# A hand-written instruction order, exchanged for the first periods of a matrix product

## The chip, the cores and the metric

The kernel runs on one core of a Trainium2 chip. The metric is the device time of one execution in microseconds (us). The engines are called as in the profile: PE multiplies matrices, DVE and ACT do elementwise work, POOL does little here, and SP issues every DMA of this kernel. Each engine works through its own list of instructions in order; an instruction that waits holds up all that stands behind it on the same engine.

## The reference

```python
def reference(x, w):
    cs = np.cumsum(x, axis=1)
    diff = cs - np.concatenate([np.zeros(...), cs[:, :-1, :]], axis=1)
    return np.matmul(diff, w).astype(np.float32)
```

x is 8 x 2048 x 2048 and w is 2048 x 2048, both float32 standard normal. The differences of a cumulative sum are the numbers that were summed, so the result is x times w: 16384 rows of 2048, each a product with the same w.

## The kernel before

**Tiles and periods.** The 16384 rows are 128 tiles of 128 rows. The first four (PLAIN = 4) are multiplied plainly, in bf16, while w is still arriving. The others go in groups of four tiles through a two-level product of the Strassen-Winograd kind in f16, which replaces matmuls on PE by additions on DVE. The work is recorded in periods: period 0 has the four plain tiles and the first group (tiles 4 to 7), period k the group of tiles 4 + 4k to 7 + 4k. Within a period a tile is called by its role: 0 to 3 are the tiles of the period's own group, 4 to 7 those of the next group, 8 and up those behind.

**Order by hand.** Every operation is first recorded with a label and an engine (L117), with no order. Then emit (L205) sorts all recorded operations by 1620 times the period plus a place, looked up by label in the table `places` (L1184 on), and each engine is given its operations in that order (after, L98). The table has an entry for periods 0, 1, 2, 29, 30 and 31, and one for all between (None). A place may be negative or over 1620: then the operation is sorted in among those of the period before or after. So the table alone sets what stands before what on PE, DVE, ACT and on SP's queue of DMAs. Waits for data follow from the tiles that are read and written.

**The head (period 0).** SP loads x tiles of the first four rows ("first x.q.a", L254; q is a quarter of the columns, a one of two pairs of rows) and w pieces ("w.h.ko", L295: half h of the columns, 128 rows ko). On DVE each x tile is cast to bf16 ("cast x", L260), PE transposes it with eight small matmuls ("turn x", L269), and DVE or ACT copies the result back ("turned x", L279). Each piece of w is cast to bf16 ("cast w", L313, on ACT) into one of seven buffers and used by the plain matmuls ("plain.h.r.ko", L324); "left over" (L476) is the last small product of that phase. Before the first data arrive, PE runs dummy matmuls on zeros ("warm", L362).

**The scale of w.** DVE takes the maximum of each piece of w ("max w", L305), then the maximum over these ("max", L447); POOL takes it over the partitions, and DVE forms uw and its reciprocal uinv (L453, L454). With uinv DVE and ACT scale w into f16 blocks B11, B21, B22 and so on (L460, L462), from which the blocks T1 to T4 and the second-level operands ("inK.make..", "inK.Q..", L576) are subtracted on DVE.

**A group's x.** For a tile of role r: load r (SP, L132), weigh r (ACT, sums of absolute values, L140), mean r (ACT, L161), scale r (DVE, reciprocal, L163), narrow r.i (ACT, to f16, L178), turn r.i (SP, a DMA that transposes from the staging buffer F into the x operands, L195). Each comes in two halves i. S1g, S1h, S2h, S3h and S4h are sums of x tiles on DVE (L576). S1h of a period subtracts the tiles of its roles 2 and 3, which are roles 6 and 7 of the period before.

**A group's products.** P1 to P5 are products with second-level operands. PN.0 to PN.6 are their quarter matmuls on PE (L610; four matmuls each) and some plain products are issued by L588. PN.s1 to PN.s4 are subtractions on DVE for operands; PN.first, PN.out2 and PN.out4 are copies on ACT (L627); PN.middle and PN.last are DVE's. Results are first kept by ACT ("keep", L624) and then added to by DVE ("C11g+P2.g.0" and the like, L635), each sum in two halves. When both halves of a sum are done, SP stores it ("put r.h", L643).

**SP.** All DMAs of the kernel stand in one queue in the order of the table. A DMA that waits, for instance a store for its sum, holds those behind it.

Of the kernel before, what the change touches and what calls it, by code (L numbers as in the profile page):

```python
# [10 lines left out]
def kernel(  # L11
# [30 lines left out]
    WARM = 30  # L42
# [72 lines left out]

    def record(label, engine, ask):
# [56 lines left out]
    def narrow_one(t, i):  # L173
        to, data, s = narrowed(t)[:, ds(i * NH, NH)], where[t][i], scales[t]
        record(
            f"narrow{role(t)}.{i}",
            "act",
            lambda: nc.scalar.activation(to, data, COPY, scale=s),  # L178
        )
        if i == 1 and t != PLAIN + 1:  # L180
            stage.append(where[t][1])
# [75 lines left out]
    def cast_x(q, a):  # L257
        to = resting(q, 0).bitcast(bf16).rearrange("p (a c) -> p a c", a=2)[:, a]
        src = resting(KH - 1 - q, a)
        record(f"cast x.{q}.{a}", "dve", lambda: nc.vector.tensor_copy(to, src))  # L260
        return to
# [13 lines left out]
    def turned(q, a, v, engine):  # L275
        to = xP[:, ds(2 * a, 2), ds(q * KQ, KQ), :].rearrange("p r k m -> p r (k m)")
        v = v.rearrange("p (r c) -> p r c", r=2)
        on = nc.scalar.copy if engine == "act" else nc.vector.tensor_copy
        record(f"turned x.{q}.{a}", engine, lambda: on(to, v))  # L279
# [30 lines left out]
    def taken(h, ko):  # L310
        src = rest(h, ko)
        to = wb[h, ko] = next(rings)
        record(f"cast w.{h}.{ko}", "act", lambda: nc.scalar.copy(to, src))  # L313
        largest(h, ko)
# [22 lines left out]
    def result(name, p, rows, columns, u=None):  # L337
        c = next(results_at)
        if u is None and name in ("out.0.1.0", "out.0.2.0"):
            record(f"{name}", "dve", lambda: nc.vector.tensor_copy(c, p))  # L340
        elif u is None:
            record(f"{name}", "act", lambda: nc.scalar.copy(c, p))  # L342
        else:
            record(f"{name}", "act", lambda: nc.scalar.activation(c, p, COPY, scale=u))
# [52 lines left out]
    for ko in range(KO - KQ):  # L397
# [20 lines left out]
        if ko == PART[-1]:  # L418
            for k in PART:
                part(k)  # L420
            record("part", "act", lambda: nc.scalar.copy(partial, banks[7]))
# [35 lines left out]
    def block(name, dst, a, h, k, engine):  # L457
        to, src = dst[k], whole[k][:, a, h, :].rearrange("p (n c) -> p n c", c=NB)
        if engine == "dve":
            ask = lambda: nc.vector.tensor_scalar(to, src, uinv, None, MUL)  # L460
        else:
            ask = lambda: nc.scalar.activation(to, src, COPY, scale=uinv)  # L462
        record(f"{name}.{k}", engine, ask)
# [159 lines left out]
    def keep_one(label, c, p, u):  # L623
        record(label, "act", lambda: nc.scalar.activation(c, p, COPY, scale=u))  # L624

    def copy(label, to, p):
        record(label, "act", lambda: nc.scalar.copy(to, p))  # L627
# [188 lines left out]

    def group_plain(g):
# [69 lines left out]
        make_2(in_2)  # L887
# [16 lines left out]
        make_3(in_3)  # L904
# [18 lines left out]
    def all_seven(g):  # L923
        return g > PLAIN + 4

# [3 lines left out]
    def first_two(g):  # L929
        if g < END:  # L930
# [3 lines left out]
            if all_seven(g):  # L934
# [3 lines left out]
            ready[2] = Quarters("P2", ready["zz"], A12g, A12h, in_2, room(at + 1), False)  # L938

    def group(g):  # L940
        h = g + 2
        more = all_seven(g)
# [30 lines left out]
        if more:  # L973
# [29 lines left out]
        P5 = Quarters("P5", P2.banks, S1g, S1h, in_5, room(at))  # L1003
# [12 lines left out]
        if not more:  # L1016
            make_5(in_5)
        in_5.give("Q3")
# [15 lines left out]
        if not more:  # L1034
            make_1(in_1)
# [7 lines left out]
        P3 = Quarters("P3", P5.banks, S4g, S4h, in_3, room(at + 1))  # L1043
# [12 lines left out]
        in_3.give("Q1")  # L1056
# [20 lines left out]
        P4 = Quarters("P4", P3.banks, A22g, A22h, in_4, room(at))  # L1077
        P4.one()
        P4.two()
        in_3.give("Q3")  # L1080
        if not more:
            make_3(in_4)
# [19 lines left out]
        in_4.give("Q1")  # L1102
# [19 lines left out]
        in_4.give("Q3")  # L1122
# [25 lines left out]
        if next_g < END:  # L1148
            if all_seven(g + 4):
# [12 lines left out]
        P4.slot(6)  # L1162
        turn(next_l, [1])
# [13 lines left out]
    for g in range(PLAIN + 4, END, 4):  # L1177
# [8 lines left out]
            'first x.0.2': 0, 'first x.1.1': 1, 'first x.0.0': 2, 'first x.1.3': 3,  # L1186
            'first x.0.3': 4, 'first x.0.1': 5, 'first x.1.2': 6, 'first x.1.0': 7, 'w.0.0': 8,
            'zeros': 9, 'least': 10, 'ones': 11, 'numbers': 12, 'numbers turned': 13, 'eye': 14,
# [394 lines left out]
```

## Time and profile before

| | |
|---|---|
| time, median of 3 runs | 1450.54 us (1450.36 to 1450.79) |
| the profiled execution's span, first to last instruction | 1449.2 us |
| its clock of PE, mean granted | 0.999 of full speed |
| DMA | 351.59 MB, mean 243 GB/s |
| instructions | 20358, of which PE 6692, DVE 2345, ACT 1994 |

The span leaves out what lies before the first and behind the last instruction; the median of the runs is 1.3 us above it. In the profile a row of the timeline gives the start in us, the time to the end of the last of its instructions, engine, line, operation, what is written from what, the count, and in brackets how long the engine was idle before the first of them and who ended that wait. A row of the windows gives for a stretch of time its length and, for each engine, the busy us with the count of instructions, then the granted clock of PE, the share of time that the DMA engines were busy, and GB/s. A row of a group gives count, busy us, the mean of one in ns, the idle time before them and who ended most of it.

The chain of work that ended last is 91% on PE: 61% on L610 and 30% on L588.

### The profile page before, as it was taken

To read this page: it belongs to the slowest core of one execution; us is meant where nothing else is said; L and a number is where in the kernel's file an instruction comes from. 1 tells how busy PE (TensorE), PEld (TensorE's weight loads), DVE (VectorE), ACT (ScalarE), POOL (GpSimd) and SP (SyncE) were. 2 spreads that over 40 slices of the span, in tenths; PEclk is the share of its full clock that TensorE was granted. 3 is DMA by queue.
4 is the path that set the end of the run, shared out by engine and by line. 5 is a ranking of instruction groups with operands and counts; after the bars stand their busy time and mean duration, and the time that the engine had idled before them with its cause. 6 is when DMAs were issued, how large, how long until landed. Compare 5 with 4: busy or idle time off the path is not lost.

```text
span 1449.2 us, 20358 instructions
## 1 busy us (share of the span) xinstructions
PE 1438.6 (99%) x6692; PEld 652.2 (45%) x6698; DVE 1334.3 (92%) x2345; ACT 1204.5 (83%) x1994; POOL 0.5 (0%) x5
## 2 busy tenths in 40 slices
PE   8999999999999999999999999999999999999998
PEld 4444444444444444444444444444444444444443
DVE  6999999999999999999999999999999999999988
ACT  5997888898888888888988888988888888889783
POOL 0000000000000000000000000000000000000000
PEclk9999999999999999999999999999999999999999
DMA  9999979899888999989998888998989998989973
GB/s 360 369 252 272 252 212 228 240 247 262 226 234 226 243 262 231 244 222 228 247 265 233 228 229 237 252 257 226 222 239 244 260 248 225 218 236 248 264 200 116
DMA packets 343930, 351.59 MB, mean 243 GB/s; under 512 B 270992, under 2 KB 270992, under 8 KB 343824
## 3 DMA queue, kind: packets, MB, share of 16 engines
q1 hardware_dynamic: 343824, 350.29, 89.4%
q8 instruction: 52, 0.85, 0.2%
q14 instruction: 54, 0.44, 0.1%
HBM read 150.99 MB, written 134.22 MB: 197 GB/s over the span
## 4 chain that ended last, share of the span: by engine, by line
PE 91%; issue 4%; DMA 2%; ACT 2%; DVE 1%; DVEq 0%; POOLq 0%; ACTq 0%; SPq 0%
PE b L610 61%; PE b L588 30%; DMA x<-F 1%; DMA F<-in_x_dram 1%; DVE W L460 1%; ACT waste L140 0%; DMA out_dram<-arena 0%; ACT W L462 0%; DVE arena L635 0%; ACT arena L624 0%; ACT F L178 0%; ACT arena L342 0%; ACT arena L178 0%; DVE arena L576 0%; DVE W L576 0%
## 5 line engine op out<-in xcount | busy, mean ns | idle before, releaser
L588 PE MATMUL b<-W,x 128*128 128x512 f16 x2144 | 518.1, 379 | 0.1
L635 DVE SCALAR_TENSOR_TENSOR arena<-b,tiny,arena 128x512 f32<-128x512 f32 x612 | 446.9, 745 | 16.0 <-PE b L610 4.8
L610 PEld LDWEIGHTS <-arena 128*128 128x128 f16 x2744 | 268.2, 98 | 325.4 <-DVE arena L576 6.3
L610 PE MATMUL b<-W,arena 128*128 128x512 f16 x1672 | 413.7, 379 | 0.8 <-DVE arena L576 0.4
L624 ACT ACTIVATE arena<-b,tiny 128x512 f32<-128x512 f32 x496 | 317.0, 684 | 35.4 <-PE b L588 14.9
L588 PEld LDWEIGHTS <-x 128*128 128x128 f16 x2144 | 209.7, 98 | 253.3 <-issue 0.3
L140 ACT ACTIVATE waste<-F,tiny 128x1024 uint8<-128x1024 f32 x246 | 283.9, 1154 | 15.6 <-DMA F<-in_x_dram 14.1
L178 ACT ACTIVATE F<-F,tiny 128x1024 f16<-128x1024 f32 x246 | 282.1, 1147 | 10.9 <-DVE tiny L163 9.4
L610 PE MATMUL b<-W,x 128*128 128x512 f16 x1192 | 287.5, 379 | 0.0
L610 PE MATMUL b<-arena 128*128 128x512 f16 x1072 | 261.6, 379 | 0.0
L610 PEld LDWEIGHTS <-x 128*128 128x128 f16 x1428 | 139.7, 98 | 168.5
L576 DVE TENSOR_TENSOR b<-b,arena 128x512 f32<-128x512 f32 x298 | 205.9, 691 | 5.7 <-ACT arena L627 2.0
L627 ACT COPY b<-b 128x512 f32<-128x512 f32 x149 | 85.5, 574 | 134.4 <-PE b L610 112.4
L627 ACT COPY arena<-b 128x512 f32<-128x512 f32 x298 | 170.2, 580 | 19.9 <-PE b L610 13.0
L576 DVE TENSOR_TENSOR arena<-W 128x2048 f16<-128x2048 f16 (+1 forms) x158 | 185.6, 1176 | 0.4 <-PE b L610 0.4
L576 DVE TENSOR_TENSOR arena<-x,x 128x512 f16<-128x512 f16 (+1 forms) x181 | 91.5, 506 | 50.1 <-PE b L610 50.1
L576 DVE TENSOR_TENSOR x<-x,x 128x1024 f16<-128x1024 f16 x124 | 85.2, 687 | 2.0
L576 DVE TENSOR_TENSOR arena<-W,arena 128x512 f16<-128x512 f16 (+1 forms) x157 | 85.9, 563 | 0.6 <-PE b L610 0.5
L576 DVE TENSOR_TENSOR arena<-arena 128x512 f16<-128x512 f16 x120 | 50.8, 424 | 13.7 <-PE b L610 11.8
L610 PE MATMUL b<-arena,x 128*128 128x512 f16 x236 | 60.3, 379 | 0.0
L324 PE MATMUL b<-arena 128*128 128x512 bf16 x234 | 53.5, 379 | 1.5 <-DVE arena L279 0.8
L576 DVE TENSOR_TENSOR arena<-x,arena 128x512 f16<-128x512 f16 x119 | 49.6, 417 | 0.6 <-PE b L610 0.6
(49 smaller groups left out, 503.6 us busy)
## 6 DMA issues: line engine op xcount, KB each, us to landing
F<-in_x_dram SPq DMA_DIRECT2D x246, 512.0 KB, 5.4
out_dram<-arena SPq DMA_DIRECT2D x240, 512.0 KB, 4.8
W<-in_w_dram SPq DMA_DIRECT2D x31, 512.0 KB, 9.5
out_dram<-arena SPq DMA_DIRECT2D x31, 256.0 KB, 2.7
W<-in_x_dram SPq DMA_DIRECT2D x16, 256.0 KB, 6.6
x<-F SPq DMA_TRANSPOSE x246, 4.4
arena<-in_x_dram SPq DMA_DIRECT2D x2, 512.0 KB, 5.1
W<-in_w_dram SPq DMA_DIRECT2D x2, 256.0 KB, 9.0
```

What stands on the lines that cost most here:

```text
L140: lambda: nc.scalar.activation(waste, data, ABS, bias=least, scale=1.0 / ROW, accum_out=m),
L178: lambda: nc.scalar.activation(to, data, COPY, scale=s),
L324: said = nc.tensor.matmul(to[n], xP[:, r, ko, :], b[:, ds(n * NB, NB)], start=(ko == 0), stop=(ko == KO - 1),)
L460: ask = lambda: nc.vector.tensor_scalar(to, src, uinv, None, MUL)
L576: record(label, "dve", lambda: nc.vector.tensor_tensor(dst, p, q, op))
L588: said = nc.tensor.matmul(to[n], a[k], b[k][:, n, :], start=(start and k == 0), stop=(k == KH - 1), skip_group_check=True,)
L610: said = nc.tensor.matmul(to, a[k], b[k], start=(start and k == 0), stop=(k == 3), skip_group_check=True)
L624: record(label, "act", lambda: nc.scalar.activation(c, p, COPY, scale=u))
L627: record(label, "act", lambda: nc.scalar.copy(to, p))
L635: label, "dve", lambda: nc.vector.scalar_tensor_tensor(c, p, u, c, MUL, ADD)
```

## The change

Three things change. (1) WARM goes from 30 to 24. (2) Twenty-four casts, copies and scalings change engine by a table `moved`, looked up when they are recorded: eight go from DVE to ACT (cast x.0.0, x.1.0, x.2.0, x.2.1, x.3.0, turned x.0.0, out.0.1.0, out.0.2.0), thirteen from ACT to DVE in period 0 (cast w.0.0, .2, .3, .5, .6, .7, .8, .9, .11, .12, cast w.1.0 and w.1.15, turned x.1.0), three from ACT to DVE in period 2 (narrow4.1, narrow6.1, one half of keep C12g). (3) The entries 0, 1 and 2 of `places` are written anew. The entries 29, 30, 31 and None stay, and from period 3 on each engine has the same order as before. `plainly` and `made` choose for each product whether it runs at one level; what they choose is what the code chose before, so the products are the same. The DMAs are the same 817.

```diff
-    WARM = 30
+    WARM = 24
...
+    moved = {
+        0: (
+            "cast x.0.0", "turned x.0.0", "cast w.0.0", "cast x.1.0", "cast w.0.2",
...
+        2: (
+            "narrow4.1", "keep C12g.1", "narrow6.1",
+        ),
+    }
+
     def record(label, engine, ask):
         at = seen[period[0], label] = seen.get((period[0], label), 0) + 1
         if at > 1:
             label = f"{label}#{at}"
+        if isinstance(ask, dict):
+            if label in moved.get(period[0], ()):
+                engine = {"act": "dve", "dve": "act"}[engine]
+            ask = ask[engine]
         ops.append((period[0], label, engine, ask))
+
+    def on_two(to, src, scale=None):
+        if scale is None:
+            return {
+                "act": lambda: nc.scalar.copy(to, src),
+                "dve": lambda: nc.vector.tensor_copy(to, src),
+            }
+        return {
+            "act": lambda: nc.scalar.activation(to, src, COPY, scale=scale),
+            "dve": lambda: nc.vector.tensor_scalar(to, src, scale, None, MUL),
+        }
...
-            lambda: nc.scalar.activation(to, data, COPY, scale=s),
+        record(f"narrow{role(t)}.{i}", "act", on_two(to, data, s))
...
-        record(f"cast w.{h}.{ko}", "act", lambda: nc.scalar.copy(to, src))
+        record(f"cast w.{h}.{ko}", "act", on_two(to, src))
...
+    def plainly(name, g):
+        return name in {PLAIN + 4: ('P1',)}.get(g, ())
```

The new table as orders. *SP, head:* x.0.0, x.0.3, x.0.2, x.0.1, x.1.1, x.1.0, w.0.1, w.0.0, w.0.2 and so on (before: eight x tiles, x.0.2 first, then w.0.0, w.0.1). *PE, head:* 20 dummies, turn x.0.1, 2 dummies, turn x.1.0, 1, turn x.0.0, 1, then plain.0.3.0 (before: 22 dummies, turn x.0.1, 7, turn x.1.0, 1, turn x.0.0, plain.0.1.0). *SP at the end of period 0:* before, load7.0, put1.1, put2.1, load7.1, turn5.0, turn5.1, load8.0, put3.1, put1.0, load8.1, turn7.0, turn7.1; after, load7.0, load8.0, load7.1, turn5.0, turn5.1, put1.0, put2.1, put3.1, load8.1, turn7.0, turn7.1, with put1.1 ahead of load7.0. *DVE in period 0:* C12h+Z.1 stands behind more work, P2.s1 ahead of more. *DVE in period 1:*

```diff
-            'C11g+P2.g.0': 494, 'C11g+P2.g.1': 495, 'P5.0': 496, 'S2g T2.1.0': 498,
-            'S2g T2.0.0': 499, 'unit4': 500, 'scale4': 504, 'C11h+P2.h.0': 505, 'P5.first': 506,
-            'S1h': 507, 'S3h': 508, 'P5.s1': 509, 'P5.s2': 510, 'P5.3': 555, 'P5.2': 556,
...
+            'S2g T2.1.0': -1331, 'keep C11h.0': -1331, 'C11g+P2.g.1': -1330, 'S1h': -1329,
+            'C11g+P2.g.0': -1328, 'put0.0': -1327, 'P5.0': -1327, 'C11h+P2.h.0': -1326,
+            'S2g T2.0.0': -1326, 'P5.s1': -1325, 'P5.first': -1325, 'S3h': -1324, 'weigh6.0': -1324,
+            'P5.3': -1324, 'scale4': -1323, 'P5.s2': -1322, 'narrow4.0': -1322, 'S2h': -1321,
```

(In the new table the places of periods 1 and 2 are negative: with 1620 added for each period they continue the count of period 0.)

More of the change, by code (lines that the diff above doesn't have):

```diff
@@ L277, in turned @@
         v = v.rearrange("p (r c) -> p r c", r=2)
-        on = nc.scalar.copy if engine == "act" else nc.vector.tensor_copy
-        record(f"turned x.{q}.{a}", engine, lambda: on(to, v))
+        record(f"turned x.{q}.{a}", engine, on_two(to, v))
     wb = {}
@@ L335, with result @@
     results_at = iter(results * 2)
-    def result(name, p, rows, columns, u=None):
+    def result(name, p, rows, columns):
         c = next(results_at)
[L339 to L344, printed above, removed]
+        record(name, "dve" if name in ("out.0.1.0", "out.0.2.0") else "act", on_two(c, p))
         done.append(
@@ L420 @@
                 part(k)
-            record("part", "act", lambda: nc.scalar.copy(partial, banks[7]))
+            record("part", "act", on_two(partial, banks[7]))
     for ko in range(KO - KQ, KO):
@@ L458, in block @@
         to, src = dst[k], whole[k][:, a, h, :].rearrange("p (n c) -> p n c", c=NB)
[L459 to L463, printed above, removed]
+        record(f"{name}.{k}", engine, on_two(to, src, uinv))
     def finish_row(r):
@@ L623, in keep_one @@
     def keep_one(label, c, p, u):
-        record(label, "act", lambda: nc.scalar.activation(c, p, COPY, scale=u))
+        record(label, "act", on_two(c, p, u))
     def copy(label, to, p):
-        record(label, "act", lambda: nc.scalar.copy(to, p))
+        record(label, "act", on_two(to, p))
     def add(label, c, p, u, halves=range(2)):
@@ L972, in group @@
         P1.slot(1)
-        if more:
+        if not P1.plain:
             in_1.give("Q4")
@@ L1002, in group @@
         P1.slot(5)
-        P5 = Quarters("P5", P2.banks, S1g, S1h, in_5, room(at))
+        if plainly("P5", g):
+            P5 = Whole("P5", P2.banks, S1g, S1h, T1)
+        else:
+            P5 = Quarters("P5", P2.banks, S1g, S1h, in_5, room(at))
         P2.slot(4)
@@ L1015, in group @@
         P1.slot(6)
-        if not more:
-            make_5(in_5)
-        in_5.give("Q3")
+        if not P5.plain:
+            made("P5", in_5, make_5)
+            in_5.give("Q3")
         C11h = keep("keep C11h", Y, uh, free.pop(1))
@@ L1033, in group @@
         total("S4g", S4g, A12g, S2g, SUB)
-        if not more:
-            make_1(in_1)
+        if not plainly("P1", g + 4):
+            made("P1", in_1, make_1)
+        if not plainly("P2", g + 4):
+            made("P2", in_2, make_2)
         go(2)
@@ L1055, in group @@
         P5.slot(4)
-        in_3.give("Q1")
+        if not P3.plain:
+            in_3.give("Q1")
         P5.last()
@@ L1076, in group @@
         P3.three()
-        P4 = Quarters("P4", P3.banks, A22g, A22h, in_4, room(at))
+        if plainly("P4", g):
+            P4 = Whole("P4", P3.banks, A22g, A22h, T4)
+        else:
+            P4 = Quarters("P4", P3.banks, A22g, A22h, in_4, room(at))
         P4.one()
         P4.two()
-        in_3.give("Q3")
-        if not more:
-            make_3(in_4)
+        if not P3.plain:
+            in_3.give("Q3")
+        if not P4.plain:
+            made("P4", in_4, make_3)
         narrow(next_h)
@@ L1101, in group @@
         P3.last()
-        in_4.give("Q1")
+        if not P4.plain:
+            in_4.give("Q1")
         scale_of(next_k)
@@ L1121, in group @@
             ready[1].two()
-        in_4.give("Q3")
+        if not P4.plain:
+            in_4.give("Q3")
         weigh(next_l, [0])
@@ L1162, in group @@
         P4.slot(6)
+        if P4.plain and not plainly("P4", g + 4):
+            made("P4", in_4, make_3)
+        if P5.plain and not plainly("P5", g + 4):
+            made("P5", in_5, make_5)
+        if P3.plain and not plainly("P3", g + 4):
+            made("P3", in_3, make_3)
         turn(next_l, [1])
@@ L1185 @@
         0: {
[L1186 to L1188 removed]
[47 rows of a table removed]
[L1236 removed]
[49 rows of a table removed]
[L1286 removed]
[41 rows of a table removed]
[L1328 removed]
[48 rows of a table removed]
[L1377 removed]
[42 rows of a table removed]
+            'ones': 1, 'first x.0.0': 1, 'numbers': 2, 'first x.0.3': 2, 'zeros': 3,
[136 rows of a table added]
+        },
[54 rows of a table added]
+        },
[47 rows of a table added]
         },
```

35 lines of the change are left out of this document (19 added, 16 removed), and 456 rows, old and new, of tables (moved, places).

## The prediction

> **What bounds it now.** I read the page's busy shares (busy us, share of the span, instructions), then windows over the first 185 us by stage, then the timelines of PE and DVE where PE has a gap, then SP's.
>
> ```profile
> PE 1438.6 (99%) x6692; PEld 652.2 (45%) x6698; DVE 1334.3 (92%) x2345; ACT 1204.5 (83%) x1994; POOL 0.5 (0%) x5
> ```
>
> The windows (their columns are in their own first line):
>
> ```profile
> core 0: us, PE busy (x) PEld busy (x) DVE busy (x) ACT busy (x) POOL busy (x), PEclk, DMA share, GB/s
> 0.00:61.00 61.00, 56.65 (x295) 26.81 (x301) 47.09 (x57) 42.78 (x48) 0.54 (x5) 1.00 0.98 380
> 61.00:107.00 46.00, 45.65 (x211) 20.38 (x210) 45.34 (x72) 42.74 (x69) 0.00 (x0) 1.00 0.98 256
> 107.00:140.00 33.00, 32.16 (x150) 14.29 (x148) 31.46 (x74) 25.52 (x41) 0.00 (x0) 1.00 1.09 279
> 140.00:185.00 45.00, 45.00 (x210) 20.38 (x209) 44.24 (x90) 38.24 (x65) 0.00 (x0) 1.00 0.88 238
> ```
>
> PE is full; from 140 us on without a gap. The change leaves every engine's order from period 3 (about 180 us) as it was, so all it can win or lose is PE time before that: the gaps of the first 140 us.
>
> ```profile
> 9.09 0.62 PE L269 MATMUL b<-waste,W 128*128 128x128 bf16 x8 [1.68 <-DVE W L260]
> ...
> 13.19 4.30 PE L324 MATMUL b<-arena 128*128 128x512 bf16 x17 [0.79 <-DVE arena L279]
> ...
> 134.70 1.89 PE L588 MATMUL b<-W,x 128*128 128x512 f16 x8
> 136.99 1.02 PE L610 MATMUL b<-W,arena 128*128 128x512 f16 x4 [0.40 <-ACT b L627]
> 138.45 1.90 PE L610 MATMUL b<-W,arena 128*128 128x512 f16 x8 [0.44 <-DVE arena L576]
> ...
> 177.31 1.89 PE L610 MATMUL b<-arena,x 128*128 128x512 f16 x8
> ```
>
> Real work starts at 13.19. A matmul costs 0.216 us ((1.89 - 0.38) / 7, with 0.38 the mean of one). The last gap is at 138.45: PE waits for P5.s2 of period 1, a subtraction on DVE. So the end is set by when DVE gets there.
>
> ```profile
> 60.77 0.16 DVE L454 RECIPROCAL tiny<-tiny 128x1 f32<-128x1 f32 x1
> ...
> 106.64 0.16 DVE L163 RECIPROCAL tiny<-tiny 128x1 f32<-128x1 f32 x1 [0.48 <-ACT tiny L161]
> ...
> 132.63 1.40 DVE L635 SCALAR_TENSOR_TENSOR arena<-b,tiny,arena 128x512 f32<-128x512 f32 x2
> 134.95 0.16 DVE L163 RECIPROCAL tiny<-tiny 128x1 f32<-128x1 f32 x1 [0.92 <-ACT tiny L161]
> 135.53 0.75 DVE L635 SCALAR_TENSOR_TENSOR arena<-b,tiny,arena 128x512 f32<-128x512 f32 x1 [0.41 <-ACT arena L624]
> 136.19 0.68 DVE L576 TENSOR_TENSOR arena<-x,x 128x1024 f16<-128x1024 f16 x1
> ...
> 137.52 0.88 DVE L576 TENSOR_TENSOR arena<-arena 128x512 f16<-128x512 f16 x2
> ```
>
> Between uinv (60.77) and P5.s2 (the second at 137.52) DVE idles only three times: 0.48 + 0.92 + 0.41 = 1.81 us. 136.19 is S1h of period 1.
>
> **The change part by part.** The same 817 DMAs and the same matmuls remain, six dummies apart.
>
> *Head.* The dummies cost nothing themselves: they end in a 1.68 us wait for the first cast. The same 2 MB (six x tiles of 256 KB, w.0.1; before eight tiles) are issued ahead of w.0.0, which lands as before at 11.5; on w.0.0 two casts follow.
>
> ```profile
> 8.34 0.69 DVE L260 CAST W<-W 128x1024 bf16<-128x1024 f32 x1 [5.08 <-DMA W<-in_x_dram]
> ```
> ```profile
> 11.57 1.05 ACT L313 CAST arena<-W 128x1024 bf16<-128x1024 f32 x1 [9.57 <-DMA W<-in_w_dram]
> 12.52 1.01 ACT L279 COPY arena<-b 128x1024 bf16<-128x1024 bf16 x1
> ```
>
> The first is DVE's, the others ACT's. The casts of x as a group (busy, mean ns, idle before):
>
> ```profile
> L260 DVE CAST W<-W 128x1024 bf16<-128x1024 f32 x8 | 5.3, 691 | 7.1 <-DMA W<-in_x_dram 7.1
> ```
>
> Before, ACT did cast and copy in series (11.57 to 13.2). Now w.0.0's cast is on DVE (0.69), beside ACT's copy of x.0.0 (cast on ACT about 10, two turns of 0.62, copy 1.01): both end near 12.5. PE starts about 0.7 earlier. In the plain phase DVE now casts ten more w pieces in their arrival order; I put 0.9 us of small new gaps against 0.8 of old ones, so PE keeps about 0.6 of lead at the end of that phase. It only waits longer for DVE later: worth 0 in the sum. Without that cover, 0.7.
>
> *DVE up to uinv.* Ahead of the global maximum of w, DVE takes over 12 casts and copies and gives up 8: +4 x 0.61 (0.69 less the overlap of two) = 2.5 us.
>
> ```profile
> L305 DVE TENSOR_REDUCE tiny<-W 128x1 f32<-128x1024 f32 x31 | 35.8, 1210 | 4.3 <-DMA W<-in_w_dram 4.2
> ```
> ```profile
> 60.58 0.15 DVE L453 TENSOR_SCALAR tiny<-tiny 128x1 f32<-128x1 f32 x1 [0.48 <-POOL tiny L451]
> ```
>
> They go into idle time: 4.3 before the maxima alone, 7.1 (5.08 of it at the very start) before the casts. The late idle is in front of the last pieces of w, whose bytes come as before, so uinv is 0 to 0.6 us earlier; I take **-0.27**. One w cast stands in the 0.48 wait for POOL.
>
> *DVE from uinv to P5.s2.* Counted instruction by instruction: 141 with 75.11 us before, 142 with 75.17 after (five 0.33 subtractions move ahead, three of them and a P2.last of 0.60 move behind). No gain there. PE's work ahead of P5.2 is equal too. The three idle times vanish: scale6 and scale4 no longer stand in front of ready work (scale4 goes behind S3h), and C11h+P2.h.0 comes later: **-1.81**, at zero new waits.
>
> *The new wait.* S1h moves ahead of C11g+P2.g.0 (132.63), on which PE's P5.0 waits. S1h needs both transposes of the x tile of role 7: turn7.0 and turn7.1.
>
> ```profile
> 112.50 1.40 DVE L635 SCALAR_TENSOR_TENSOR arena<-b,tiny,arena 128x512 f32<-128x512 f32 x2
> ...
> 120.02 0.41 DVE L576 TENSOR_TENSOR arena<-x 128x512 f16<-128x512 f16 x1
> ```
>
> These are C22+X.0 with C12h+Z.1, and P2.s1 of period 1. SP's queue, and what the trace gives for turn7.0 and turn7.1:
>
> ```profile
> 122.45 0.90 SPq L643 DMA_DIRECT2D out_dram<-arena  x2
> ...
> 124.87 0.34 SPq L132 DMA_DIRECT2D F<-in_x_dram  x1
> 125.52 7.49 SPq L195 DMA_TRANSPOSE x<-F  x2
> ```
>
> ```profile
> L195 SPq DMA_TRANSPOSE x<-F x2: 1992/3692/5393, 125.5 to 127.6; - x2
> ...
> DMA to landing us min/median/max: 8.1/8.4/8.6
> ```
>
> Turn7.1, issued from 127.6, lands 8.1 later: 135.7. S1h at 136.19 didn't feel it, scale4 and C11h stood in the way. Now DVE is ready for S1h at 136.19 - 1.81 - 0.27 - 1.77 (its work ahead falls from 73.74 to 71.97) = 132.3 to 132.4. When does turn7.1 land? The set of DMAs in front is the same, but load8.0 goes ahead of turn5 (before: right ahead of turn7), so one 512 KB load less is still in flight. The median of all transposes from 60 to 140 us:
>
> ```profile
> x<-F SPq DMA_TRANSPOSE x14, 6.0
> ```
>
> At the 279 GB/s of the window 107 to 140 us, 512 KB is 1.9 us; at the 380 of the first window 1.4. So 133.8 to 134.3 if all of that counts, 135.7 if none. By the other side: a store now ahead of the turns, put2.1, waits for C12h+Z.1, which on DVE moves from 113.2 (the second at 112.50) to about 121.4; its issue at 122.4, plus the 13.3 from 122.45 to turn7.1's landing at 135.7, less 1.4 to 1.9, is 133.8 to 134.3 too, and up to 135.7 by its worse end. I take 134.7, in the middle: a wait of 134.75 - 132.4 = **+2.35**. C11g+P2.g.0 and, through it, P5.0 on PE stand behind. P2.s1 moves from 120.02 to about 112.7. It needs turn6.1, whose place a product on PE frees at about 109.3, and which lands some 3.1 to 4.9 later; in the same view for 110 to 113 us the old one, issued at 110.4, took 4.7:
>
> ```profile
> DMA to landing us min/median/max: 4.7/5.3/5.9
> ```
>
> So 112.4 to 114.2: a stall of 0 to 1.5, hidden by S1h's larger one (DVE only arrives later at the same wait); without that cover it costs itself. At P5.2 the balance is -0.27 - 1.81 + 2.35 = +0.27. With no wait it would be -2.1. PE's own work would stop it near -2.3: 0.6 of lead, and the idle of the windows from 61 to 140 us (0.35 + 0.84, with 0.16 more for each of three gaps, as a matmul's 0.38 outlasts its step): 1.7.
>
> *P5.s2 to period 2.* Until the subtraction that P1.6 of period 2 waits for, DVE's work rises from 38.04 to 41.21 us (three subtractions more ahead and work put off from period 1), +3.17; PE has two more products of 4 matmuls ahead, +1.73.
>
> ```profile
> 172.39 0.70 DVE L576 TENSOR_TENSOR b<-b,arena 128x512 f32<-128x512 f32 x1 [0.24 <-issue]
> ...
> 174.06 0.43 DVE L576 TENSOR_TENSOR arena<-x,arena 128x512 f16<-128x512 f16 x1 [0.31 <-PE b L610]
> ...
> 176.01 1.08 DVE L576 TENSOR_TENSOR arena<-W,arena 128x512 f16<-128x512 f16 x3
> ```
>
> Of the 1.44 between them, 0.22 were spare (released at 177.09, the end of the last row; started at 177.31) and up to 0.66 of DVE idle, mostly the two shown, can be filled: +0.56 to +1.22, I take **+0.9**.
>
> *Three ops to DVE in period 2* (two narrows, one keep). The trace has the form of the narrows on DVE (the scaling of w):
>
> ```profile
> L460 DVE TENSOR_SCALAR W<-W,tiny 128x1024 f16<-128x1024 f32 x18 | 12.2, 748 | 0.1
> ```
>
> It takes 0.75 (step 0.66): 2.0 us, and stands behind the place of the +0.9; 0 to 0.3, taken as 0: what PE waits for behind that place comes with no less to spare.
>
> Sum: -0.27 - 1.81 + 2.35 + 0.9 = +1.2. The span of 1449.2 becomes 1450.4; the median of the runs is 1.3 above it, so **1451.7 us**. From period 3 on nothing changes.
>
> **Rivals.** *Faster: no wait at S1h.* If turn7.1 lands by 132.4, the sum is -2.1 + 0.9 = -1.2: 1449.3; with P1.6's term at its low end 1449.0. For it: the window's median landing of 6.0, 2.1 under the 8.1 here, gives 133.6 with the old issue, hence 132.4 if load8.0's place also advances the issue. Against: put2.1 in front. *Slower: the store holds SP.* put2.1 waits on SP for C12h+Z.1, with put3.1, load8.1 and both turns of role 7 behind it. If P2.s1 stalls 1.5 and C12h+Z.1 slips to 123, put2.1 issues 1 later than before and takes 13.3 from there: landing 137.3, +2.6 on the sum: 1454.3. It decides from a landing of 133.5 (the sum is zero there); every us of landing is one us of time, so 136.4 makes it slower by over 0.2%. *A slow clock at the head.* Fewer dummies ahead of the first matmuls:
>
> ```profile
> 0.00:4.00 4.00, 2.83 (x7) 1.00 0.41 109
> 4.00:8.00 4.00, 3.41 (x16) 1.00 0.94 292
> ```
>
> The first dummies take 0.40 each (2.83 / 7), those after 4 us 0.21. The old idle of 1.68 us didn't bring the slow step back. If a longer one did, and it lasted as at the start (1.17 to 4 us), 7 matmuls would cost 0.2 more each, 1.4 us, inside the 2.6 that PE has to spare at P5.2 (0.27 + 2.3); at three times that length it would be 4.2 - 2.6 = +1.6: 1453.3. [...]
>
> **How the numbers follow.** A measurement here tells about 0.2% (2.9 us) from none: 1447.6 and 1453.4. Chances: forecast (landing 133.5 to 136.4) 0.50; no wait 0.20; the store 0.24; the clock 0.06. Faster by 0.2% would need nearly all old gaps gone with no wait: 0.06. Slower: the store (0.24) and, 0.08, the forecast's upper end (+1.3 at a landing of 135.7, 1.22 and 0.3: +2.8, at the bound): 0.32. The range 1448.6 to 1455.2 goes from the faster rival less 0.7 (the head's lead kept) to the store rival plus 0.9 (0.3 each for uinv no earlier, P1.6's upper end, the three ops).
>
> **What would show it.** Right: first matmul of L324 near 12.5; uinv near 60.5; DVE idle of 1 to 3.5 us in front of S1h, released by a transpose; P5.2 at 138.5 to 139; P1.6 near 178; tails alike. Wrong: no DMA wait there; a longer issue stall in SP's row of stores at 122; or new PE gaps before 69 us of over 2.

## The result and the profile after

| | runs | median us | range |
|---|---|---|---|
| before | 5 | 1450.36 | 1449.52 to 1450.79 |
| changed | 5 | 1454.24 | 1453.00 to 1456.64 |

The ratio is 1.003 (95% interval 1.0019 to 1.0042): 3.9 us slower. That lies inside the predicted range (1448.6 to 1455.2), 2.5 us above the predicted time. The changed kernel's runs scatter over 3.6 us, those of before over 1.3.

The profile of the changed kernel was taken of its slowest run (span 1454.8 us). First the busy shares, then the windows by stage, whose columns are those shown before:

```profile
PE 1440.5 (99%) x6692; PEld 652.4 (45%) x6692; DVE 1338.8 (92%) x2353; ACT 1194.8 (82%) x1986; POOL 0.5 (0%) x5
```
```profile
0.00:61.00 61.00, 55.83 (x286) 26.36 (x287) 49.10 (x59) 36.42 (x41) 0.54 (x5) 0.94 0.99 380
61.00:107.00 46.00, 44.48 (x206) 19.91 (x205) 43.17 (x68) 40.32 (x64) 0.00 (x0) 1.00 0.98 241
107.00:140.00 33.00, 31.53 (x144) 13.87 (x142) 30.09 (x72) 24.69 (x42) 0.00 (x0) 1.00 1.07 264
140.00:185.00 45.00, 44.28 (x205) 19.95 (x205) 44.85 (x92) 35.59 (x60) 0.00 (x0) 1.00 0.89 239
```

Two things are new. The granted clock of the first window is 0.94, where it was 1.00. And DVE, 45.34 busy in the second window before, has only 43.17: it waits where it didn't. The windows of the head show the clock:

```profile
8.00:10.00 2.00, 1.04 (x10) 0.54 (x9) 1.09 (x3) 1.77 (x3) 0.00 (x0) 1.00 1.02 408
10.00:12.00 2.00, 1.10 (x11) 0.82 (x12) 0.97 (x1) 0.85 (x1) 0.00 (x0) 0.82 1.02 402
12.00:14.00 2.00, 1.34 (x10) 0.86 (x9) 1.31 (x3) 0.62 (x1) 0.00 (x0) 0.50 1.04 386
14.00:16.00 2.00, 1.56 (x4) 0.56 (x4) 1.62 (x3) 1.34 (x2) 0.00 (x0) 0.50 1.04 411
16.00:18.00 2.00, 2.00 (x6) 0.76 (x5) 0.40 (x1) 0.00 (x0) 0.00 (x0) 0.50 1.05 381
```

From about 11 to 18 us PE runs at half clock (0.50; four matmuls take 1.56 us from 14 to 16). From 8 to 12 us PE had been busy for 2.1 of 4 us, mostly with small transposes (18 of its 21 matmuls). What it does to DVE, in the timeline (start, time, operation, in brackets the idle time before and who ended it):

```profile
59.97 0.19 DVE L464 TENSOR_REDUCE tiny<-tiny 128x1 f32<-128x33 f32 x1
61.68 0.69 DVE L142 CAST arena<-W 128x1024 bf16<-128x1024 f32 x1 [1.53 <-PE b L346]
62.29 0.15 DVE L470 TENSOR_SCALAR tiny<-tiny 128x1 f32<-128x1 f32 x1
62.47 0.16 DVE L471 RECIPROCAL tiny<-tiny 128x1 f32<-128x1 f32 x1
```

The maximum comes at 59.97 as before (59.91). But the cast of w.1.15, which the change put on DVE in front of uw, needs a bf16 buffer that a late matmul of the plain phase (L346) holds, and uinv moves from 60.77 to 62.47. Later on DVE, S1h of period 1 (L589, third row) waits for a transpose, with C11g+P2.g.0 behind it, as the prediction had it; PE's P5.0 waits for that:

```profile
135.79 1.22 DVE L589 TENSOR_TENSOR arena<-W 128x2048 f16<-128x2048 f16 x1
136.93 0.74 DVE L648 SCALAR_TENSOR_TENSOR arena<-b,tiny,arena 128x512 f32<-128x512 f32 x1
139.31 0.69 DVE L589 TENSOR_TENSOR arena<-x,x 128x1024 f16<-128x1024 f16 x1 [1.65 <-DMA x<-F]
139.92 0.74 DVE L648 SCALAR_TENSOR_TENSOR arena<-b,tiny,arena 128x512 f32<-128x512 f32 x1
```
```profile
140.72 1.02 PE L623 MATMUL b<-W,arena 128*128 128x512 f16 x4 [1.65 <-DVE arena L648]
```

P5.2 starts at 143.30 instead of 138.45. One execution can't tell how much of this is the clock of this run, so the kernel was run again.

### The profile page after: what moved, and what is told of

The parts are those of the page before. It is cut to its first block, busy times and chain, and to the rows that moved or that the text cites. A ratio compares the mean times of both kernels' runs of the same rounds, so it can differ in the third digit from the quotient of the medians.

```text
span 1454.8 us, 20361 instructions
## 1 busy us (share of the span) xinstructions
PE 1440.5 (99%) x6692; PEld 652.4 (45%) x6692; DVE 1338.8 (92%) x2353; ACT 1194.8 (82%) x1986; POOL 0.5 (0%) x5
## 4 chain that ended last, share of the span: by engine, by line
PE 94%; DMA 3%; ACT 2%; DVE 1%; issue 0%; SPq 0%; DVEq 0%; ACTq 0%
PE b L623 61%; PE b L601 29%; PE b L346 4%; DMA x<-F 2%; DMA F<-in_x_dram 1%; ACT F L145 1%; DMA W<-in_x_dram 0%; ACT waste L167 0%; DVE arena L648 0%; PE b L292 0%; ACT arena L141 0%; ACT arena L145 0%; DVE arena L589 0%; ACT W L145 0%; SPq L277 0%
## 5 line engine op out<-in xcount | busy, mean ns | idle before, releaser
L648 DVE SCALAR_TENSOR_TENSOR arena<-b,tiny,arena 128x512 f32<-128x512 f32 x612 | 447.4, 745 | 17.2 <-ACT arena L141 4.6
L141 ACT COPY arena<-b 128x512 f32<-128x512 f32 (+1 forms) x319 | 184.4, 589 | 35.5 <-PE b L623 12.4
L589 DVE TENSOR_TENSOR b<-b,arena 128x512 f32<-128x512 f32 x298 | 205.7, 691 | 5.1 <-ACT arena L141 1.5
L589 DVE TENSOR_TENSOR arena<-W 128x2048 f16<-128x2048 f16 (+1 forms) x158 | 185.7, 1175 | 0.2 <-PE b L623 0.2
L589 DVE TENSOR_TENSOR arena<-x,x 128x512 f16<-128x512 f16 (+1 forms) x181 | 91.5, 506 | 52.6 <-PE b L623 50.1
L589 DVE TENSOR_TENSOR x<-x,x 128x1024 f16<-128x1024 f16 x124 | 85.1, 687 | 1.9
L589 DVE TENSOR_TENSOR arena<-W,arena 128x512 f16<-128x512 f16 (+1 forms) x157 | 86.0, 563 | 0.2 <-PE b L623 0.2
L589 DVE TENSOR_TENSOR arena<-arena 128x512 f16<-128x512 f16 x120 | 50.8, 424 | 13.7 <-PE b L623 11.8
L346 PE MATMUL b<-arena 128*128 128x512 bf16 x240 | 55.1, 388 | 1.1 <-ACT arena L141 1.1
L589 DVE TENSOR_TENSOR arena<-x,arena 128x512 f16<-128x512 f16 x119 | 49.5, 416 | 0.3 <-PE b L623 0.3
```

Of the source, the lines that this page charges most:

```text
L141: "act": lambda: nc.scalar.copy(to, src),
L346: said = nc.tensor.matmul(to[n], xP[:, r, ko, :], b[:, ds(n * NB, NB)], start=(ko == 0), stop=(ko == KO - 1),)
L589: record(label, "dve", lambda: nc.vector.tensor_tensor(dst, p, q, op))
L648: label, "dve", lambda: nc.vector.scalar_tensor_tensor(c, p, u, c, MUL, ADD)
```

## The experiments

The time before on the same chips was 1449.9 to 1450.1 us in four sets of runs, 95 in all. "Clear median" leaves out the runs whose mean granted clock was 0.998 or less. "DVE idle" is the length of the window from uinv's end to P5.s2's start less DVE's busy time in it, in the profiled run.

| run | what it is | median us | ratio to before (95%) | clear median | uinv | DVE idle |
|---|---|---|---|---|---|---|
| again | the change | 1453.20 | 1.0026 (1.0015 to 1.0037) | 1452.9 | 60.90 | 3.84 |
| dummies | six more dummies | 1453.23 | 1.0019 (1.0011 to 1.0028) | 1453.2 | 62.45 | 4.62 |
| w115 | cast of w.1.15 behind uinv | 1453.66 | 1.0027 (1.0016 to 1.0038) | 1453.3 | 60.93 | 4.24 |
| s1h | S1h put back | 1453.41 | 1.0023 (1.0014 to 1.0033) | 1453.4 | 60.97 | 3.05 |
| before_again | the kernel before | 1450.12 | 1.0002 (0.9993 to 1.0011) | 1450.1 | 60.16 | 0.59 |
| head_only | changed up to uinv | 1450.32 | 1.0006 (0.9997 to 1.0015) | 1450.0 | 61.12 | 0.53 |
| rest_only | changed behind uinv | 1453.38 | 1.0025 (1.0016 to 1.0033) | 1453.2 | 60.39 | 4.23 |
| load7 | load8.0, weigh4.0 put back | 1453.28 | 1.0024 (1.0015 to 1.0032) | 1453.2 | 60.50 | 3.00 |
| early60 | six places put back | 1454.14 | 1.0029 (1.0018 to 1.0041) | 1453.1 (3 runs) | 63.37 | 4.01 |
| mid_before | 61 to 88 us as before | 1452.59 | 1.0017 (1.0008 to 1.0026) | 1452.6 | 61.35 | 3.17 |
| front_after | changed up to S1g only | 1451.68 | 1.0014 (1.0005 to 1.0023) | 1451.7 | 61.55 | 1.60 |
| together | dummies, early60, load7, s1h | 1452.18 | 1.0015 (1.0006 to 1.0024) | 1452.2 | 61.09 | 3.13 |

### The change again

No edit. 

> The changed kernel once more, nothing edited, so that the others have a neighbour on the same chip. Its five times so far lie from 1453.0 to 1456.6 us. Theory A (the head: a half clock around 11 to 18 us makes PE late, and a cast of w on DVE that stands in front of uw waits for PE, so that uinv comes at 62.5 instead of 60.8) expects the spread to be that of the clock: a profile without the half clock has uinv below 61.5 and a span near 1451, one with it has uinv above 62 and a span of 1453 or more. Theory B (the transposes: S1h of period 1 waits for turn7.1, whatever the head does) expects a DVE wait of 1 to 3 us at S1h in every profile and the spread from DMA landings.

Seven runs: five from 1452.69 to 1453.83 us, and two at 1455.93 and 1456.71, with a mean clock of 0.997. The profiled run (1452.94, span 1451.2) is one of the five, and its first real matmul comes at 13.09 with the clock at 1.00. So the change costs some 3 us in the runs with a mean clock of 0.999 or more, and another 3 to 4 in the two runs with the low mean clock. In the clear profile uinv comes at 60.90, and DVE waits here (four rows out of the timeline):

```profile
84.64 0.75 DVE L648 SCALAR_TENSOR_TENSOR arena<-b,tiny,arena 128x512 f32<-128x512 f32 x1 [1.17 <-ACT arena L145]
85.54 0.69 DVE L589 TENSOR_TENSOR arena<-x,x 128x1024 f16<-128x1024 f16 x1 [0.16 <-DMA x<-arena]
...
125.96 0.16 DVE L190 RECIPROCAL tiny<-tiny 128x1 f32<-128x1 f32 x1 [0.51 <-ACT tiny L188]
...
136.21 0.69 DVE L589 TENSOR_TENSOR arena<-x,x 128x1024 f16<-128x1024 f16 x1 [1.72 <-DMA x<-F]
```

They are C11g+V.1 (for a keep on ACT, which stands there behind the two halves of weigh3), S1g (for turn1.1), scale7 (for mean7) and S1h (for turn7.1): 3.56 us. Three wait for x on its way through load, weigh, scale, narrow and turn, the first for an ACT that had waited for a load; only the last was forecast.

PE, the engine whose gaps make the time, waits in three places from 60 to 185 us, and the first two of these waits are not for DVE (rows out of the timeline):

```profile
75.90 7.08 PE L601 MATMUL b<-W,x 128*128 128x512 f16 x32 [1.26 <-DMA x<-F]
83.51 3.63 PE L601 MATMUL b<-W,x 128*128 128x512 f16 x16 [0.53 <-DMA x<-F]
...
137.62 1.02 PE L623 MATMUL b<-W,arena 128*128 128x512 f16 x4 [1.73 <-DVE arena L648]
```

The first two wait for transposes of the group's own x: turn0.1 is issued at 68.01 and lands at 75.8, turn2.1 is issued at 77.23 and lands at 83.4 (in the second profile of the kernel before, shown below, they land at 73.3 and 79.0). Only the third wait, P5.0's behind S1h, lies on the way that the prediction followed.

Theory A, the clock, explains the two slowest of these seven runs, though not every slow one: of the first five, the run at 1455.52 has a mean clock of 1.00. Theory B has its wait at S1h, which is about half of the idle time.

### Six dummies more

```diff
-    WARM = 24
+    WARM = 30
...
-            'warm.21': 26,
+            'warm.21': 26, **{f'warm.{i}': 26.5 for i in range(24, 30)},
```

> The changed kernel with 30 dummies again: six more between the first two groups of transposes at the head, where PE was idle for 1.4 us. Theory A: no half clock between 8 and 18 us, first matmul of the plain phase near 13.3, PE's lateness at the end of the plain phase gone, uinv at 60.5 to 61.2, time 1450.5 to 1452.5, spread under 1 us. Theory B: head better, but the wait at S1h takes what is won there; time within 0.7 of the unedited one.

No run of 11 has a mean clock under 0.999, and the clear median is that of the unedited change: theory A had the median wrong. Its spread of under 1 us didn't come either. Ten runs lie from 1451.94 to 1453.78; the eleventh, 1455.44, is the profiled one, with a clock of 1.00 from 8 to 18 us, and yet the maximum over w comes at 61.24 and uinv at 62.45. So a late uinv also comes about without the half clock. Counted over all kernels here with the changed head and 24 dummies, 15 of 80 runs have a mean clock of 0.998 or less; with 30 dummies (this one and the last) none of 22; the kernel before 4 of 95, none of them above 1452, and rest_only, with the old head, 1 of 11. (Only the profiled ones of these show where the clock was halved.)

### The cast of w.1.15 behind uinv

```diff
-            'plain.1.0.11': 145, 'plain.1.3.8': 146, 'plain.1.3.9': 147, 'cast w.1.15': 147,
+            'plain.1.0.11': 145, 'plain.1.3.8': 146, 'plain.1.3.9': 147, 'cast w.1.15': 149.5,
```

> The changed kernel with the cast of w.1.15 on DVE moved from in front of uw to right behind uinv. Theory A: uinv at 60.7 to 61.0 whatever the clock, as DVE no longer waits for PE there; the 1.5 us come back at the end where the half clock happens, time 1451.5 to 1453. Theory B: uinv earlier, wait at S1h longer by as much, time as the unedited one within 0.7.

Uinv at 60.93, and no gain: in a clear run there is nothing for the cast to wait for (it sits in the wait for POOL, as forecast), and two of the eight runs had the low mean clock and were at 1455.56 and 1456.95 all the same. So the slow runs don't need the way through this cast.

### S1h put back

```diff
-            'S2g T2.1.0': -1331, 'keep C11h.0': -1331, 'C11g+P2.g.1': -1330, 'S1h': -1329,
+            'S2g T2.1.0': -1331, 'keep C11h.0': -1331, 'C11g+P2.g.1': -1330, 'S1h': -1325.5,
```

> The changed kernel with S1h of period 1 moved back behind C11g+P2.g.0 and C11h+P2.h.0 on DVE. Theory B: 1.3 to 1.7 us of DVE work now stand in front of the wait for turn7.1, the wait shrinks from 1.65 to under 0.3, P5.2 and the end come 1.3 to 1.7 us earlier: the unedited time less 1.5. Theory A: P5.0 comes earlier, but the lateness from the head stays; at most 0.5 us less.

The wait at S1h is gone, P5.2 starts at 139.35 instead of 140.21, and the time doesn't fall. In this profile DVE still idles for 3.05 us: 0.59 at C11g+V.1, 0.62 at scale5, 0.99 at scale7, and 0.31 at C11h+P2.h.0; and PE still waits for transposes at 75.58 (0.44) and 83.25 (0.59). Theory B's figure of 1.5 was wrong: the place of S1h alone is not what the time hangs on.

### The kernel before once more

> The kernel before once more, unedited, for a second profile. The profiled span of 1449.2 us lies 0.8 above what the median of its 25 later times means in span (1450.1 less 1.75). Expected: span 1448.0 to 1449.2; DVE between uinv and P5.s2 idle for 1.5 to 2.2 us again, at scale4 and C11h+P2.h.0; the difference to the first profile lies before uinv, in when the first tiles land.

Here DVE does not idle at the three places on which the prediction counted. The same place of the timeline as in the prediction's rows at 132.63 to 137.52:

```profile
131.82 1.40 DVE L635 SCALAR_TENSOR_TENSOR arena<-b,tiny,arena 128x512 f32<-128x512 f32 x2
133.14 0.15 DVE L163 RECIPROCAL tiny<-tiny 128x1 f32<-128x1 f32 x1
133.31 0.75 DVE L635 SCALAR_TENSOR_TENSOR arena<-b,tiny,arena 128x512 f32<-128x512 f32 x1
133.97 0.68 DVE L576 TENSOR_TENSOR arena<-x,x 128x1024 f16<-128x1024 f16 x1
```

scale4 follows with no wait named, C11h+P2.h.0 right behind it. In the first profile load8.1 had landed at 133.27, here at 131.03, and weigh4.1 and mean4 came before DVE did. So 1.81 us of idle time were an accident of one execution. The expectation had them come back. PE, too, waits only once from 60 to 185 us in this profile:

```profile
85.50 3.63 PE L588 MATMUL b<-W,arena 128*128 128x512 f16 x16 [0.25 <-DVE arena L576]
```

It does not wait for P5.s2. A shorter way of DVE to that place had no more than these 0.25 us of PE's time to win.

### The head alone, the rest alone

Both are the changed kernel with another order for a part: `ahead` lists the labels up to uinv, which are issued first; the rest follows the other table.

```diff
+    ahead = {l: i for i, l in enumerate(ahead)}
...
+            if at == 0 and label in ahead:
+                return -10000 + ahead[label]
```

> The changed kernel's head (24 dummies, the new order on all four engines and the new engines of the casts, up to uinv on DVE) with the order of the kernel before behind it. Theory L (the loss is the later landing of turn7.1, made by the order of period 0 behind uinv): uinv within 0.7 of 60.8, time as the kernel before within 0.8, except in the one run in six where the half clock comes (3 us more). Theory H (the head loses): 1 us or more over the kernel before in undisturbed runs too.

> The reverse: 30 dummies and the head in the order and on the engines of the kernel before, the changed order from uinv on. Theory L: 2.3 to 3.3 us over the kernel before, S1h waits for turn7.1 by 1 us or more, no half clock and no run above 1455. Theory H: at most 1 us over the kernel before.

The split is clean: the head alone is the kernel before (with four of 11 runs at low clock and 1451.2 to 1452.5), the rest alone is the whole loss. The windows from uinv to P5.s2, one for each kernel, in this order: before, before_again, head_only, again, rest_only:

```profile
60.93:137.97 77.04, 76.29 (x351) 34.00 (x350) 74.77 (x141) 66.67 (x107) 0.00 (x0) 1.00 1.03 266
```
```profile
60.33:135.75 75.42, 75.17 (x349) 33.76 (x347) 74.83 (x140) 66.76 (x109) 0.00 (x0) 1.00 1.02 274
```
```profile
61.28:136.64 75.36, 74.88 (x347) 33.59 (x346) 74.83 (x141) 66.04 (x107) 0.00 (x0) 1.00 1.03 270
```
```profile
61.06:139.48 78.42, 74.74 (x343) 33.35 (x343) 74.58 (x142) 65.44 (x106) 0.00 (x0) 1.00 1.03 264
```
```profile
60.55:139.21 78.66, 75.86 (x349) 33.68 (x348) 74.43 (x142) 65.82 (x108) 0.00 (x0) 1.00 1.04 266
```

The first number after the window is its length; of the pairs of busy time and instructions behind it the third is DVE's. DVE's work is the same everywhere within 0.4 us; the length differs by its idle time alone: 0.5 to 0.6 in the usual run of the old order, 3.8 to 4.2 in the changed one. The difference, 3.3 to 3.7, is close to the loss of time: 3.1 for the change (1453.2, the median of its nine clear runs in both sets, less 1450.1) and 3.2 for the rest alone. PE's share of these windows, the first of the pairs, says the same: idle for 0.75, 0.25 and 0.48 us in the old order, for 3.68 and 2.80 in the changed one.

### Load 7 in its old place

```diff
-            'S3h T3.0.1': 236, 'load7.0': 237, 'A22g T4.0.0': 237, 'load8.0': 238,
+            'S3h T3.0.1': 236, 'load7.0': 237, 'A22g T4.0.0': 237, 'load8.0': 245.5,
...
-            'in5.make2.3': -1349, 'in4.make1.1': -1347, 'S1g': -1346, 'weigh4.0': -1346,
+            'in5.make2.3': -1349, 'in4.make1.1': -1347, 'S1g': -1346, 'weigh4.0': -1344.5,
```

> The changed kernel with the load of tile role 8 (load8.0) back behind load7.1 on SP and with weigh4.0 back behind narrow7.1 on ACT, so that the chain load7.1, weigh7.1, mean7, scale7, narrow7.1, turn7.1 is as before. Theory L: load7.1 is issued about 1 us earlier and lands 1 to 2 earlier, narrow7.1 comes 2 to 3 earlier, turn7.1 lands 1 to 2.5 earlier, the wait at S1h falls from 1.7 under 0.7, time 1451.3 to 1452.3. Rival (DVE's other new waits, at C11g+V.1 and for the scales, set the end): within 0.4 of the unedited one.

The chain behaves as expected. ACT in the clear profile of the change, then with the edit (weigh7.1, mean7, narrow7.0, narrow7.1):

```profile
124.31 1.15 ACT L167 ACTIVATE waste<-F,tiny 128x1024 uint8<-128x1024 f32 x1 [1.45 <-DMA F<-in_x_dram]
...
125.65 0.28 ACT L188 ACTIVATE tiny<-tiny 128x1 f32<-128x1 f32 x1
...
126.40 1.14 ACT L145 ACTIVATE F<-F,tiny 128x1024 f16<-128x1024 f32 x1
...
128.57 1.14 ACT L145 ACTIVATE F<-F,tiny 128x1024 f16<-128x1024 f32 x1
```
```profile
122.44 1.15 ACT L167 ACTIVATE waste<-F,tiny 128x1024 uint8<-128x1024 f32 x1 [0.18 <-DMA F<-in_x_dram]
...
125.38 2.33 ACT L145 ACTIVATE F<-F,tiny 128x1024 f16<-128x1024 f32 x2 [0.75 <-DVE tiny L190]
```

In the change ACT waits 1.45 for load7.1, because load8.0 goes first, and weigh4.0 stands between the two narrows; turn7.1 is issued at 129.79, 0.08 behind the end of narrow7.1. With the edit narrow7.1 ends 2.0 us earlier, turn7.1 lands at 134.78 instead of 136.12, and the wait at S1h is 0.34. The profiled run (1451.71) is the fastest of its 11. Yet their clear median is 1453.2, no better than the change: nothing that can be measured was won. PE's waits for transposes at 75 and 83 us are still there (0.79 and 0.56).

### Six places at 60 to 80 us

```diff
-            'put out.0.2.0': 172, 'put out.0.1.1': 173, 'load3.0': 174, 'load3.1': 175,
-            'narrow2.1': 179, 'turn2.1': 180,
+            'put out.0.2.0': 113.3, 'put out.0.1.1': 113.6, 'load3.0': 170.5, 'load3.1': 171.5,
+            'narrow2.1': 170.7, 'turn2.1': 171.7,
```

(The places stand in several lines of the table; here they are drawn together.) The reason was seen in the windows from 60 to 70 us, of before_again, then of rest_only, which have the same head (the last two numbers are the DMA engines' share and GB/s):

```profile
60.00:70.00 10.00, 10.00 (x48) 4.52 (x47) 9.86 (x19) 9.87 (x17) 0.00 (x0) 1.00 0.98 307
```
```profile
60.00:70.00 10.00, 10.00 (x48) 4.50 (x47) 9.66 (x18) 9.23 (x16) 0.17 (x1) 1.00 0.72 240
```

The change takes two stores out of this stretch, puts them between turn2.0 and load3.0, and so leaves the DMA engines idle for a quarter of it, while they are full in the ten us before and behind it (shares of 1.03 and 1.15 in rest_only). 

> The changed kernel with six places of period 0 put back behind uinv: the stores of out.0.2.0 and out.0.1.1 ahead of turn0.0 on SP, load3.0 ahead of turn2.0, load3.1 and turn2.1 right behind it, and narrow2.1 right behind narrow2.0 on ACT (in the change it stands behind two scalings of w and weigh1). Theory S (the chain of x through SP and ACT falls behind at 60 to 80 us, where DMA stands idle, and never catches up, so DVE waits for it at whichever of C11g+V.1, the scales, S1g and S1h of period 1 comes latest): DMA share at 60 to 70 us 0.95 or more, turn2.1 lands at 79 to 81 instead of 83, turn1.1 at 83 instead of 85, turn7.1 1.5 to 3 earlier, DVE's new waits sum to under 1.5 instead of 3.5, time 1450.5 to 1452. Rival (order behind 100 us, load8.0 ahead of load7.1 and put1.1 ahead of load7.0): turn2.1 earlier, but turn7.1 within 0.7 of 135 to 136 and time 1452.5 or more.

Inconclusive: three of six runs had the low mean clock, among them the profiled one, whose clock is 0.85 from 8 to 14 us and 0.59 from 14 to 20. The other three (1451.79, 1453.13, 1453.31) show no gain. In the profile DVE's wait at C11g+V.1 is gone and one of 1.85 at scale1 has come.

### The stretches between

> The changed kernel with, on all four engines, the order of the kernel before between uinv and S1g (some 61 to 88 us), the changed head ahead of it and the changed order behind it. Theory S: 1 us or less over the kernel before, turn7.1 at 133.5 to 134.5. Rival: 2.3 to 3.3 us over it as without the edit.

> The complement: the changed order up to S1g, the order and engines of the kernel before behind it. Theory S: 2 us or more over the kernel before, with DVE waiting for the same chain of x in the old order. Rival (order behind 100 us): at most 1 us over the kernel before.

Theory S doesn't have it, and the rival only half. With the stretch from uinv to S1g as before, the change still costs 2.7 us against its own before-runs, as the rival said; with the order changed only up to S1g it costs 1.8, where the rival had at most 1. The parts overlap: together they would be 4.5, and the change costs 3.1. PE's idle time from uinv to P5.s2 follows them, with 2.75 and 1.87 us beside 3.68 in the change. In front_after all of it lies before 88 us: PE waits twice for transposes (0.30 and 0.50) and once, for 1.07, for an addition on DVE (L648 in the change). In mid_before 2.16 of DVE's 3.17 us of idle time stand at the forecast place:

```profile
133.01 0.74 DVE L650 SCALAR_TENSOR_TENSOR arena<-b,tiny,arena 128x512 f32<-128x512 f32 x1
135.91 0.69 DVE L591 TENSOR_TENSOR arena<-x,x 128x1024 f16<-128x1024 f16 x1 [2.16 <-DMA x<-F]
```

DVE is there early, as it had waited little before (0.56 at scale7), and waits 2.16 for turn7.1. So the order behind S1g suffices for most of the loss, and the last wait there is S1h's. It hides another: at 133.97 PE had waited 1.53 for a copy on ACT, which stood behind a keep that waited 1.59 for a store.

### Four edits together

The diffs of dummies, s1h, load7 and early60 in one kernel. 

> The changed kernel with four edits at once, of which each alone gave nothing clear: 30 dummies, the six places of period 0 at 60 to 80 us, load8.0 behind load7.1 with weigh4.0 behind narrow7.1, and S1h of period 1 behind C11h+P2.h.0. Theory S+L (DVE's waits for the chain of x stand in for one another: take one away and the next takes its place, and only with all gone does the time fall): DVE's waits between uinv and P5.s2 sum to under 1.2 instead of 3.3, P5.2 77 to 77.5 after uinv instead of 79.3, no half clock, time 1450.3 to 1451.5. Rival (something else in the changed order costs the 3 us, such as PE's or DVE's order between 88 and 140 us): within 0.7 of 1453.1.

1452.18 us with no run above 1453.07: 1.0 less than the change, half of what was expected. Two other waits have come, at scale1 and at S1g of period 1 (for turn5.1):

```profile
77.17 0.16 DVE L190 RECIPROCAL tiny<-tiny 128x1 f32<-128x1 f32 x1 [1.47 <-ACT tiny L188]
...
127.31 0.69 DVE L589 TENSOR_TENSOR arena<-x,x 128x1024 f16<-128x1024 f16 x1 [1.41 <-DMA x<-F]
```

PE waits for a transpose at 76.09 (0.71), for DVE at 131.01 (0.92) and at 139.19 (0.17). Every edit agrees with waits that stand in for one another, but DVE's were never all gone (3.13 here, where theory S+L had under 1.2), so the theory was not put to its test. Which places between uinv and 140 us would have to go back to win the other 2 us stays open. No version found is faster than the kernel before.

## Why the prediction was nearly right, and where it failed

*What bounds the kernel:* right that PE is full and that only its gaps in the first 140 us count; in the clear profile of the change PE is busy for 45.00 of 45.00 us from 140 to 185 us. But that DVE's arrival at P5.s2 sets the end held for the first profile of the kernel before alone; in the second PE never waits for it.

*Head, PE 0.7 earlier, worth 0:* the 0.7 did not come (13.09 in the clear profile, 13.19 before; 13.0 to 14.0 in the others without the half clock); worth 0 was right.

*uinv -0.27:* wrong in sign. With the changed head and a clear clock it came at 60.50 to 61.55 in eight profiles, 62.45 in one, with the old head at 60.16 to 60.77. These tenths cost little: the head alone costs nothing that can be measured.

*Equal DVE work from uinv to P5.s2:* right, 74.58 against 74.77 and 74.83.

*-1.81 from the three idle times:* this is the step that failed. The count was made against one profiled execution, whose idle time was 2.27; the second has 0.59, and PE waits there for 0.25 in all. As far as two profiles tell, the kernel before has no such time to give in its usual run. Taking a stall in a single trace as a gain made up 1.8 of the 1.9 to 2.7 us by which the forecast change of +1.2 fell short (3.1 between clear medians, 3.9 in the first runs).

*+2.35 at S1h:* the mechanism was right, the size short. turn7.1 lands at 136.1, not 134.7: the sum counted the DMAs in front of it, but it waits for narrow7.1, and that for load7.1 behind load8.0. And DVE lost time at C11g+V.1 and scale7 on its way, where no wait was foreseen; S1h would have taken that up, since its transpose is late. All new idle time comes to 3.3 (3.84 less 0.59), where the term had 2.35.

*PE's own work ahead of P5.2:* taken as equal and never held up, without a look at SP's order between 60 and 90 us. In the clear profile PE waits there for turn0.1 and turn2.1, 1.79 us in all, before DVE's wait at S1h matters. front_after has these early waits alone and loses 1.8; in the whole change they overlap with S1h's.

*+0.9 at P1.6:* not there. PE comes later to P1.6 (180.83 in the clear profile instead of 177.31) and finds its operand ready.

*The sum by what was measured:* 0 for uinv, 0 for the old idle times, +3.3, 0 for P1.6: 3.3, beside 3.1 between clear medians. That the forecast came no further off was in part luck: the waits that were sized 0.95 too short and the 0.9 at P1.6 that didn't come cancel, and the range is 6.6 us wide.

*The rivals.* The store's time, 1454.3, was hit by the median of the first five runs, by other causes: in the clear profile put2.1 was issued at 124.78, 1.3 us after C12h+Z.1 had ended, and turn7.1 waited for narrow7.1. The half clock, given 0.06 and at most +1.6, comes in about one run in five (15 of 80), if the low mean clock counts it rightly. Such runs are 2 to 4 us longer in the changed kernel and its variants, 1.3 to 2.5 with the changed head alone. In the two profiles that show it (the first of the change, and early60's) it passes through the cast of w.1.15 to uinv, a way that the prediction had written off as hidden in the wait for POOL; but the runs of w115, without that way, paid as much, so by what way it costs the rest stays open. That a longer idle stretch would bring a slow clock, and for three times as long as the slow dummies at the start (0.40 us each, at a granted clock of 1.00), was the author's estimate, and no run shows it. The clock fell to 0.50 behind idle stretches of PE of 1.40 us at most in the first profile (in early60's PE idles for 2.76 us in all from 8 to 14 us), and stayed at 1.00 behind 1.55 us in again's and 1.90 us in s1h's. What sets it off was not shown.

## What to carry to other kernels

A stall in one trace is not yet a gain to be had: profile the kernel before a second time, and count only idle time that comes back, on the engine that sets the time as well as on the one that feeds it. Where an engine waits at several places for one chain of loads, conversions and transposes, removing one wait can move the time to the next (here the 1.72 us at S1h went, and the clear median was 1453.4, beside 1453.2 for the change); ask when the chain itself is done, by its longest path, not how many transfers stand in front of one transfer. An early operation moved ahead of ready work is only as good as the latest thing that it waits for.

## What the runs showed of the hardware

In the first profile of the changed kernel PE ran at half clock (0.50) from about 11 to 18 us. From 8 to 12 us it had been busy for 2.1 of 4 us, mostly with transposes (18 of its 21 matmuls), and it had not been idle for more than 1.4 us at once. Such a stretch doesn't decide it alone: in the profile of s1h PE was busy for 2.05 of the same 4 us, idle for 1.90 us at once, and kept its full clock (1.00). With six dummies of 0.22 us between two groups of transposes none of 22 runs had a low mean clock, without them 15 of 80. Such a run can be the one that is profiled, as it was here first.
